# S5's entering states by one instruction for both directions, turned by ScalarE; a late bias on ScalarE; a pad of 448 bytes

## The chip, the cores and the metric

The kernel runs on one core of a Trainium2 chip. The metric is the device time of one execution in microseconds (us), the median of several runs. TensorE (PE) multiplies and loads weights (PEld), VectorE (DVE) and GpSimd (POOL) do elementwise work, ScalarE (ACT) does activations and copies, and SyncE (SP) issues nearly all DMAs. On-chip memory (SBUF) has 128 partitions; a tile is a rectangle in it. PE writes into PSUM banks, which ACT and DVE empty.

## The reference

One layer of a diffusion backbone for 256 context tokens and 2048 latent tokens, width 1024. Two parts of it matter here, S5 and the matrix products.

```
def s5_scan(u, a_re, a_im, log_dt, b_re, b_im, c_re, c_im, s0_re, s0_im):
    ...
    a_cum, h = lax.associative_scan(compose, (a_seq, bu), axis=1)
    h = h + a_cum * lax.complex(s0_re, s0_im)[:, None]
    y = jnp.einsum('gcp,btgp->btgc', lax.complex(c_re, c_im), h).real
    return y, h[:, -1]

def trunk_layer(x, cond, hg_s0, s5_s0_re, s5_s0_im, P, l):
    ada = jnp.dot(jax.nn.silu(cond), P['ada_w'][l]) + P['ada_b'][l]
    sh1, sc1, g1, sh2, sc2, g2 = jnp.split(ada[:, None, :], ADA_CHUNKS, axis=-1)
    h = rms_norm(x, P['norm1_g'][l]) * (1.0 + sc1) + sh1
    mix, hg_end, s5_re, s5_im = token_mixing(h, hg_s0, s5_s0_re, s5_s0_im, P, l)
    x = x + g1 * mix
    h = rms_norm(x, P['norm2_g'][l]) * (1.0 + sc2) + sh2
    x = x + g2 * jnp.dot(jnp.square(jax.nn.relu(jnp.dot(h, P['mlp_w1'][l]))), P['mlp_w2'][l])
```

`s5_mixer` calls `s5_scan` once forwards and once on the flipped sequence, for 16 groups of 16 channels with a complex state of 64. `token_mixing` ends in a product with `w_out`.

## The kernel before

Tokens go in five blocks: block 0 is the 256 context tokens, blocks 1 to 4 are 512 latent tokens each. Every large product is split in three: an operand is held as a rounded `hi` and a remainder `lo`, and `gemm_cm` (lines 186 to 194) issues hi by hi, lo by hi and hi by lo for each of 8 slices of the width, 24 matmuls into one PSUM bank. One such bank is called a unit below. Its weights (`whl`, four buffers) are loaded by `load_unit`, rounded by ACT (L156), and the remainder is subtracted by DVE (L162) or POOL (L160). The moving operand, which is streamed through PE, is a pair of `hi` and `lo` tiles of 128 by 512.

The program has three stages. Until about 700 us, pass 1 makes the normalised inputs and the recurrent part HGRN2, and the S5 tables. From about 700 to 1070 us four things share the engines: `pass2` (the rest of the input products), `s5_ctx` and `s5_lat` (S5), `ada_late` (16 of the 24 adaLN chunk pairs, which aren't needed at the start), and the output product and MLP of block 0. After that the MLP of block 0 ends and blocks 1 to 4 follow: each has `mix_out` (8 units with `w_out`, each emptied by DVE at L1225), and four quarters of `mlp_up` (8 units, emptied by ACT at L1241, squared by DVE at L1242, split by ACT at L1244 and DVE at L1245) and `mlp_down` (8 units, emptied by DVE at L1257 with the same kind of instruction as L1225).

Where the moving operands lie: pass 1 and 2 keep theirs in the pool `hp`, block 0's MLP in `h30`. In blocks 1 to 4, `mix_out` and `mlp_up` read theirs from the pool `h3a`, and `mlp_down` reads the hidden layer from `h3b`. `h3a` stands on the left side of memory behind a tile called `pad`, which nothing reads; `h3b`, `h30` and `hp` are placed from the right side. In the program as built, each 512-wide tile of `h3a` starts 1600 bytes past a multiple of 2048 within its partition (the first at byte 134,720), and each of `hp` and `h3b` starts 1984 bytes past one.

`s5_lat` does one of 16 groups at a time (lines 967 to 1023). Partitions 0 to 63 carry the forward direction, 64 to 127 the backward one, which ACT turned round when it emptied PSUM (L990, L991), so that both scan forwards. Per group: POOL makes phase tables (L322 to L327), DVE rotates the input by four products and two sums (L997, L1001, L1002), scans real and imaginary part (L1005), DVE and POOL rotate back (L997). Then `hh`, the state that enters each step, is written: DVE copies the first state for each direction (L1010, L1011), and for real and imaginary part one subtraction or addition for each half of the partitions (L1013, L1014), the lower one with a reversed order. PE multiplies `hh` with the output tables (L1018 to L1020), ACT empties that into `yl` (L1021).

`ada_unit` multiplies the condition with one pair of adaLN chunks into the only bank of `pb` (L647), ACT copies the rows (L650), PE turns them (L652), and DVE adds the bias into `adaT` (L653). Only then is the bank free for the next unit or for another user.

The engines' queues run in order. The order of all instructions on each engine is set when the program is built, by the framework's scheduler from a simulated timeline, so an edit in one place can move others around it.

Of the kernel before, what the change touches and what calls it, by code (L numbers as in the profile page):

```python
# [10 lines left out]
F32 = mybir.dt.float32  # L11
F32R = mybir.dt.float32r
I32 = mybir.dt.int32
AF = mybir.ActivationFunctionType
# [20 lines left out]
JL = LAT // S5L  # L35
# [39 lines left out]
def trunk_kernel(ctx, tc, I, O):  # L75
# [12 lines left out]
    def nm(s):  # L88
        uid[0] += 1
        return f"{s}_{uid[0]}"  # L90
# [7 lines left out]
    def pb():  # L98
        return psums["b"].tile([128, 512], F32, tag="pb", name=nm("pb"))
# [19 lines left out]
    adab = const("adab", [128, 48], I["ada_b"], q=A)  # L119
# [421 lines left out]
    def ada_late(ap_):  # L541
        c32 = cond32(ap_)
        for q in range(16):
            aws = []
            for r in range(2):
                aw = ap_.tile([128, 4, 256], F32, tag="awt", name=nm("awt"), bufs=2)
                SP.dma_start(aw, I["ada_w1"][q, :, 4 * r:4 * r + 4, :])
                aws.append(aw)
            ada_unit(pb(), aws, c32, ap_, slice(16 + 2 * q, 18 + 2 * q))
            if q == 11:  # L550
                for c in range(2):
                    V.scalar_tensor_tensor(gs2[:, c, :], adaT[:, 32:40, c], 1.0, n2g, ALU.add, ALU.mult)
            yield
# [85 lines left out]
        G.tensor_copy(c32[:, :, 0:2], csil)  # L639
        return c32  # L640

    def ada_unit(pt, aws, c32, rpool, blocks):


        for r in range(2):
            for j in range(4):
                PE.matmul(pt[32 * j:32 * j + 32, 0:256], c32[:, 4 * r + j, :], aws[r][:, j, :],  # L647
                          start=r == 0, stop=r == 1)
        row = rpool.tile([128, 256], F32, tag="row", name=nm("row"))
        A.activation(row, pt[:, 0:256], AF.Copy)  # L650
        for j in range(2):
            PE.matmul(pt[:, 256 + 2 * j:258 + 2 * j], row[:, j * 128:(j + 1) * 128], sel, start=True, stop=True)  # L652
        V.tensor_tensor(adaT[:, blocks, :], pt[:, 256:260].rearrange("p (j c) -> p j c", j=2),  # L653
                        adab[:, blocks].unsqueeze(2).to_broadcast([128, 2, 2]), ALU.add)

# [294 lines left out]
    def s5_lat(sp, s0):  # L950
# [4 lines left out]
        for q in range(4):  # L955
# [10 lines left out]
            for gq in range(4):  # L966
# [27 lines left out]
                def rot(a, dve):  # L994
                    m = [w(f"m{i}", 1 if i < 3 else 2) for i in range(4)]
                    for i, (x, y_) in enumerate(((0, pr), (1, pi), (1, pr), (0, pi))):
                        (V if i in dve else G).tensor_tensor(m[i], a[:, x, :], y_, ALU.mult)  # L997
                    return m
# [5 lines left out]
                for ri in range(2):  # L1004
                    V.tensor_tensor_scan(gg[:, ri, :], rt8[:, g:g + 1].to_broadcast([128, JL]), m[2 * ri],  # L1005
                                         s0[:, ri, g:g + 1], ALU.mult, ALU.add)
                m = rot(gg, ROT[1])
                hh = sp.tile([128, 2, JL], F32, tag="hh", name=nm("hh"), bufs=2)
                e = JL - 1
                V.tensor_copy(hh[0:64, :, 0], s0[0:64, :, g])  # L1010
                V.tensor_copy(hh[64:128, :, e], s0[64:128, :, g])  # L1011
                for ri, (x, y_, op) in enumerate(((m[0], m[1], ALU.subtract), (m[2], m[3], ALU.add))):
                    V.tensor_tensor(hh[0:64, ri, 1:JL], x[0:64, 0:e], y_[0:64, 0:e], op)  # L1013
                    V.tensor_tensor(hh[64:128, ri, 0:e][:, ::-1], x[64:128, 0:e], y_[64:128, 0:e], op)  # L1014
                ps = pdd()
                for a in range(2):
                    as_ = slice(128 * a, 128 * a + 128)
# [282 lines left out]
    def pool(stack, name, bufs=1, side="left"):  # L1300
        return stack.enter_context(tc.tile_pool(name=name, bufs=bufs, side=side))
# [179 lines left out]
    p3 = pool(e5, "p3")  # L1481
    with ExitStack() as e:
        s5_out(1, pool(e, "so1"))
    pad = pool(e5, "pad").tile([128, 16], F32, tag="pad", name="pad")
    G.memset(pad, 0.0)
    h3a = pool(e5, "h3a", 9)
    fs = mlp_up(0, 3, h2, p30, h30, none)
# [129 lines left out]
```

## Time and profile before

| | us |
|---|---|
| median of 3 runs | 2869.47 |
| lowest, highest | 2864.01, 2870.82 |
| profiled execution | 2862.84 |
| its span | 2860.9 |
| PE busy in the span | 2708.4 (95%) |
| DVE busy | 1887.5 (66%) |
| ACT busy | 1108.4 (39%) |

The span runs from the first to the last instruction of the profiled execution. PE's busy share counts pipelined matmuls, so a busy PE isn't yet a PE at its peak: how many matmuls it gets through in a stretch has to be read beside it. From 1400 us on PE is busy without a break until the last block's end; idle time lies before about 1400 us.

### The profile page before, as it was taken

To read this page: it belongs to the slowest core of one execution; us is meant where nothing else is said; L and a number is where in the kernel's file an instruction comes from. 1 tells how busy PE (TensorE), PEld (TensorE's weight loads), DVE (VectorE), ACT (ScalarE), POOL (GpSimd) and SP (SyncE) were. 2 spreads that over 40 slices of the span, in tenths; PEclk is the share of its full clock that TensorE was granted. 3 is DMA by queue.
4 is the path that set the end of the run, shared out by engine and by line. 5 is a ranking of instruction groups with operands and counts; after the bars stand their busy time and mean duration, and the time that the engine had idled before them with its cause. 6 is when DMAs were issued, how large, how long until landed. Compare 5 with 4: busy or idle time off the path is not lost.

```text
span 2860.9 us, 38042 instructions
## 1 busy us (share of the span) xinstructions
PE 2708.4 (95%) x14376; PEld 2257.5 (79%) x14376; DVE 1887.5 (66%) x2766; ACT 1108.4 (39%) x1710; POOL 920.4 (32%) x809
## 2 busy tenths in 40 slices
PE   6798999899999879999999999999999999999998
PEld 3576878887777679987788888788887888888888
DVE  9879678956899976669873475943474334543336
ACT  4645455532333445442422343333343223423323
POOL 4435334612533533343231232211332111411113
PEclk8899999999999979999999999999999999999999
DMA  7784555688886756533333343333343234233333
GB/s 264 282 294 151 188 193 178 229 286 310 299 295 225 241 173 203 174 118 111 111 103 96 125 143 108 111 99 104 114 149 106 99 94 127 90 124 96 96 96 126
DMA packets 186279, 467.17 MB, mean 163 GB/s; under 512 B 40176, under 2 KB 70000, under 8 KB 173040
## 3 DMA queue, kind: packets, MB, share of 16 engines
q1 hardware_dynamic: 183936, 463.56, 48.8%
q8 instruction: 114, 1.87, 0.3%
q10 hardware_dynamic: 2160, 1.18, 0.1%
q14 instruction: 69, 0.57, 0.1%
HBM read 383.47 MB, written 77.53 MB: 161 GB/s over the span
## 4 chain that ended last, share of the span: by engine, by line
PE 62%; DVE 10%; DMA 2%; issue 1%; ACT 0%; SPq 0%; POOL 0%; DVEq 0%; ACTq 0%
PE pg L194 20%; PE pg L193 20%; PE pg L192 20%; DVE x L1184 3%; DVE m L997 1%; DVE whl L162 1%; DMA awt<-in_ada_w_dram 1%; DVE gg L1005 1%; DVE pa L289 0%; PE pb L1051 0%; DVE hh L1014 0%; DVE hh L1013 0%; DVE lo L304 0%; DMA t<-mixD 0%; PE pd L986 0%
## 5 line engine op out<-in xcount | busy, mean ns | idle before, releaser
L192 PE MATMUL pg<-hi,whl 128*128 128x512 f32 (+1 forms) x3488 | 1286.5, 371 | 10.2 <-ACT st L586 4.9
L194 PE MATMUL pg<-hi,whl 128*128 128x512 f32 (+1 forms) x3488 | 1286.2, 370 | 8.4 <-DVE whl L162 8.4
L193 PE MATMUL pg<-lo,whl 128*128 128x512 f32 (+1 forms) x3488 | 1287.0, 370 | 2.3 <-DVE lo L1245 2.3
L160 POOL TENSOR_TENSOR whl<-wraw,whl 128x512 fp32r<-128x512 f32 (+1 forms) x296 | 435.7, 1493 | 1193.5 <-ACT whl L156 1159.9
L192 PEld LDWEIGHTS pg<-hi,whl 128*128 128x128 f32 x3488 | 662.3, 190 | 130.6 <-issue 5.8
L194 PEld LDWEIGHTS pg<-hi,whl 128*128 128x128 f32 x3488 | 662.9, 190 | 125.8 <-DVE whl L162 8.9
L193 PEld LDWEIGHTS pg<-lo,whl 128*128 128x128 f32 x3488 | 663.4, 190 | 120.0 <-issue 6.9
L156 ACT ACTIVATE whl<-wraw 128x1024 fp32r<-128x1024 f32 (+1 forms) x396 | 415.3, 1051 | 588.1 <-PE pg L194 457.0
L162 DVE TENSOR_TENSOR whl<-wraw,whl 128x1024 fp32r<-128x1024 f32 x248 | 310.7, 1254 | 63.1 <-ACT whl L156 61.8
L1257 DVE SCALAR_TENSOR_TENSOR x<-pg,adaT,x 128x512 f32<-128x512 f32 (+1 forms) x168 | 111.8, 669 | 282.9 <-PE pg L194 282.4
L1242 DVE TENSOR_TENSOR t<-t 128x512 f32<-128x512 f32 (+1 forms) x160 | 114.1, 714 | 261.0 <-ACT t L1241 260.3
L1241 ACT ACTIVATE t<-pg 128x512 f32<-128x512 f32 (+1 forms) x160 | 88.7, 554 | 382.3 <-PE pg L194 379.6
L1184 DVE SCALAR_TENSOR_TENSOR x<-x,cvw 128x512 f32<-128x512 f32 (+1 forms) x300 | 216.3, 764 | 0.6
L1245 DVE TENSOR_TENSOR lo<-t,hi 128x512 fp32r<-128x512 f32 (+1 forms) x160 | 142.5, 891 | 35.0 <-ACT hi L1244 34.8
L791 POOL TENSOR_TENSOR kt<-kt,tnx 64x256 f32<-64x256 f32 (+1 forms) x120 | 100.9, 848 | 163.6 <-issue 126.4
L252 POOL TENSOR_TENSOR sq<-sq,sq 128x512 f32<-128x512 f32 (+1 forms) x56 | 87.3, 1559 | 125.6 <-ACT sq L248 125.6
L1244 ACT ACTIVATE hi<-t 128x512 fp32r<-128x512 f32 (+1 forms) x160 | 92.8, 581 | 82.1 <-DVE t L1242 82.1
L1225 DVE SCALAR_TENSOR_TENSOR x<-pg,adaT,x 128x512 f32<-128x512 f32 (+1 forms) x40 | 27.8, 694 | 110.9 <-PE pg L194 110.8
L248 ACT ACTIVATE sq<-x 128x512 f32<-128x512 f32 (+1 forms) x120 | 66.0, 553 | 75.9 <-DVE sq L252 17.4
L787 PE MATMUL psc<-qzr,kt 128*128 128x128 f32 x576 | 74.6, 281 | 10.7 <-DVE kt L791 7.0
L787 PEld LDWEIGHTS psc<-qzr,kt 128*128 128x128 f32 x576 | 70.4, 196 | 14.4 <-POOL kt L791 7.8
L303 ACT ACTIVATE hi<-hm,adaT 128x512 fp32r<-128x512 f32 (+1 forms) x72 | 49.5, 697 | 68.5 <-DVE hm L301 64.5
(373 smaller groups left out, 2919.6 us busy)
## 6 DMA issues: line engine op xcount, KB each, us to landing
wraw<-in_mlp_w_dram SPq DMA_DIRECT2D x328, 512.0 KB, 3.5
whl<-w_p2c_hl SPq DMA_DIRECT2D x32, 1024.0 KB, 7.6
whl<-w_p1c_hl SPq DMA_DIRECT2D x22, 1024.0 KB, 7.7
wraw<-in_w_out_dram SPq DMA_DIRECT2D x40, 512.0 KB, 3.6
awt<-in_ada_w_dram SPq DMA_DIRECT2D x32, 512.0 KB, 5.9
whl<-w_p1t_hl SPq DMA_DIRECT2D x12, 1024.0 KB, 4.9
x<-in_xT_dram SPq DMA_DIRECT2D x16, 512.0 KB, 6.4
aw<-in_ada_w_dram SPq DMA_DIRECT2D x8, 1024.0 KB, 7.2
```

The source lines that it names most:

```text
L156: A.activation(hi[:, :w], raw[:, :w], AF.Copy)
L160: G.tensor_tensor(lo[:, h_], raw[:, h_], f32(hi[:, h_]), ALU.subtract)
L162: V.tensor_tensor(lo[:, :w], raw[:, :w], f32(hi[:, :w]), ALU.subtract)
L192: PE.matmul(ps[:, :n], wh, xh[:, ts], start=k == 0, stop=False)
L193: PE.matmul(ps[:, :n], wh, xl[:, ts], start=False, stop=False)
L194: PE.matmul(ps[:, :n], wl, xh[:, ts], start=False, stop=k == 7)
L787: PE.matmul(sc[:, s_], kt[:, s_], z[:, s_], start=True, stop=True)
L791: eng.tensor_tensor(kv, kv, tb(lo_, hi_, 1 - half)[:, hs_, :], ALU.mult)
L1184: V.scalar_tensor_tensor(acc[i][:, :n], u2[:, i, k:k + n], cvw[:, i, k:k + 1], acc[i][:, :n], ALU.mult, ALU.add)
L1242: V.tensor_tensor(r, r, r, ALU.mult)
L1245: V.tensor_tensor(lo, r, f32(hi), ALU.subtract)
L1257: V.scalar_tensor_tensor(x8[:, o, ts], ps[:, :n], adaT[:, 40 + o, c:c + 1], x8[:, o, ts], ALU.mult, ALU.add)
```

## The change

In `s5_lat` a new tile `sq` (in the two buffers of the tag `d`, which `d2` and `gg` use as well) takes the entering states of both directions in scan order: ACT copies the first state (one instruction), DVE does one subtraction and one addition over all 128 partitions. Two copies by ACT bring it into `hh`, the upper half turned round. DVE has 2 instructions per group where it had 6; ACT has 3 more.

`ada_unit` gets an argument for the engine. `ada_late` passes ACT, which adds the bias by two activations (one per chunk) in place of DVE's one addition. The first 8 units stay as they were.

The tile `pad` grows from 64 to 448 bytes per partition. That moves `h3a` up by 384 bytes: in the changed program its 512-wide tiles start 1984 bytes past a multiple of 2048 (the first at byte 135,104), as those of `hp` and `h3b` do in both programs. No other moving operand moves, and the order of instructions doesn't depend on it.

```diff
@@ -546,7 +546,7 @@
                 aw = ap_.tile([128, 4, 256], F32, tag="awt", name=nm("awt"), bufs=2)
                 SP.dma_start(aw, I["ada_w1"][q, :, 4 * r:4 * r + 4, :])
                 aws.append(aw)
-            ada_unit(pb(), aws, c32, ap_, slice(16 + 2 * q, 18 + 2 * q))
+            ada_unit(pb(), aws, c32, ap_, slice(16 + 2 * q, 18 + 2 * q), A)
             if q == 11:
                 for c in range(2):
                     V.scalar_tensor_tensor(gs2[:, c, :], adaT[:, 32:40, c], 1.0, n2g, ALU.add, ALU.mult)
@@ -639,7 +639,7 @@
         G.tensor_copy(c32[:, :, 0:2], csil)
         return c32
 
-    def ada_unit(pt, aws, c32, rpool, blocks):
+    def ada_unit(pt, aws, c32, rpool, blocks, eng=None):
 
 
         for r in range(2):
@@ -650,6 +650,10 @@
         A.activation(row, pt[:, 0:256], AF.Copy)
         for j in range(2):
             PE.matmul(pt[:, 256 + 2 * j:258 + 2 * j], row[:, j * 128:(j + 1) * 128], sel, start=True, stop=True)
+        if eng is A:
+            for j, o in enumerate(range(blocks.start, blocks.stop)):
+                A.activation(adaT[:, o, :], pt[:, 256 + 2 * j:258 + 2 * j], AF.Identity, bias=adab[:, o:o + 1])
+            return
         V.tensor_tensor(adaT[:, blocks, :], pt[:, 256:260].rearrange("p (j c) -> p j c", j=2),
                         adab[:, blocks].unsqueeze(2).to_broadcast([128, 2, 2]), ALU.add)
 
@@ -1005,13 +1009,15 @@
                     V.tensor_tensor_scan(gg[:, ri, :], rt8[:, g:g + 1].to_broadcast([128, JL]), m[2 * ri],
                                          s0[:, ri, g:g + 1], ALU.mult, ALU.add)
                 m = rot(gg, ROT[1])
+
+                sq = sp.tile([128, 2, JL], F32, tag="d", name=nm("sq"), bufs=2)
                 hh = sp.tile([128, 2, JL], F32, tag="hh", name=nm("hh"), bufs=2)
                 e = JL - 1
-                V.tensor_copy(hh[0:64, :, 0], s0[0:64, :, g])
-                V.tensor_copy(hh[64:128, :, e], s0[64:128, :, g])
+                A.activation(sq[:, :, 0], s0[:, :, g], AF.Copy)
                 for ri, (x, y_, op) in enumerate(((m[0], m[1], ALU.subtract), (m[2], m[3], ALU.add))):
-                    V.tensor_tensor(hh[0:64, ri, 1:JL], x[0:64, 0:e], y_[0:64, 0:e], op)
-                    V.tensor_tensor(hh[64:128, ri, 0:e][:, ::-1], x[64:128, 0:e], y_[64:128, 0:e], op)
+                    V.tensor_tensor(sq[:, ri, 1:JL], x[:, 0:e], y_[:, 0:e], op)
+                A.activation(hh[0:64], sq[0:64], AF.Copy)
+                A.activation(hh[64:128], sq[64:128, :, ::-1], AF.Copy)
                 ps = pdd()
                 for a in range(2):
                     as_ = slice(128 * a, 128 * a + 128)
@@ -1481,7 +1487,7 @@
     p3 = pool(e5, "p3")
     with ExitStack() as e:
         s5_out(1, pool(e, "so1"))
-    pad = pool(e5, "pad").tile([128, 16], F32, tag="pad", name="pad")
+    pad = pool(e5, "pad").tile([128, 112], F32, tag="pad", name="pad")
     G.memset(pad, 0.0)
     h3a = pool(e5, "h3a", 9)
     fs = mlp_up(0, 3, h2, p30, h30, none)
```

The built programs differ in their order only between about 710 and 1200 us of the run. On DVE, towards the end of S5: `gg` is the scan, `m` its rotated parts, `hh` and `sq` the entering states, `whl` a weight split, `x` and `pg` the output product of block 0, `adaT` the bias. Lines from 650 on stand up to 6 lower in the numbering after the change. Before:

```order
L1005 SCALAR_TENSOR_TENSOR gg_9116<-rt_132,s_5238,m_1409_9106 128x256
L1005 SCALAR_TENSOR_TENSOR gg_9116<-rt_132,s_5238,m_1411_9108 128x256
L997 TENSOR_TENSOR m_1414_9119<-gg_9116,ph_9087 128x256
L1225 SCALAR_TENSOR_TENSOR x_1337_8789<-pg_9173,adaT,x_1337_8789 128x256
L997 TENSOR_TENSOR m_1415_9120<-gg_9116,ph_9087 128x256
L653 TENSOR_TENSOR adaT<-pb_8491,adab 128x4
L162 TENSOR_TENSOR whl_9463<-wraw_9461,whl_9463 128x1024
L1013 TENSOR_TENSOR hh_9127<-m_1414_9119,m_1415_9120 64x255
L1014 TENSOR_TENSOR hh_9127<-m_1414_9119,m_1415_9120 64x255
L1013 TENSOR_TENSOR hh_9127<-m_1416_9121,m_1417_9122 64x255
L1014 TENSOR_TENSOR hh_9127<-m_1416_9121,m_1417_9122 64x255
```

After:

```order
L1231 SCALAR_TENSOR_TENSOR x_1349_8805<-pg_9189,adaT,x_1349_8805 128x256
L1009 SCALAR_TENSOR_TENSOR gg_9132<-rt_132,s_5238,m_1422_9122 128x256
L252 TENSOR_TENSOR sq_9221<-sq_9221,sq_9238 128x256
L1009 SCALAR_TENSOR_TENSOR gg_9132<-rt_132,s_5238,m_1424_9124 128x256
L162 TENSOR_TENSOR whl_9479<-wraw_9477,whl_9479 128x1024
L1001 TENSOR_TENSOR m_1427_9135<-gg_9132,ph_9103 128x256
L1001 TENSOR_TENSOR m_1428_9136<-gg_9132,ph_9103 128x256
L252 TENSOR_TENSOR sq_9221<-sq_9221,sq_9241 128x256
L1018 TENSOR_TENSOR sq_9143<-m_1429_9137,m_1430_9138 128x255
L1018 TENSOR_TENSOR sq_9143<-m_1427_9135,m_1428_9136 128x255
```

The bias of an adaLN unit stood on DVE between the rotation and a weight split, and is gone; four half-width instructions have become two of full width, further ahead of the next group.

The same place on ACT: `row` is an adaLN unit, `u`, `d` and `yl` are S5's input, rotated input and output. Before:

```order
L650 ACTIVATE row_8500<-pb_8491 128x256
L156 ACTIVATE whl_9463<-wraw_9461 128x1024
L983 ACTIVATE u_9341<-pd_9338 128x256
L248 ACTIVATE sq_9225<-x_1337_8789 128x256
L990 ACTIVATE d_9346<-pd_9343 64x512
L991 ACTIVATE d_9346<-pd_9343 64x512
L650 ACTIVATE row_8647<-pb_8638 128x256
L1021 ACTIVATE yl_8933<-pd_9134 128x16x16
```

After:

```order
L248 ACTIVATE sq_9238<-x_1349_8805 128x256
L156 ACTIVATE whl_9479<-wraw_9477 128x1024
L1016 ACTIVATE sq_9143<-s_5238 128x2
L987 ACTIVATE u_9357<-pd_9354 128x256
L248 ACTIVATE sq_9241<-x_1349_8805 128x256
L994 ACTIVATE d_9362<-pd_9359 64x512
L995 ACTIVATE d_9362<-pd_9359 64x512
L269 ACTIVATE rcol_9247<-pa_9244,epsb 128x2
L1019 ACTIVATE hh_9144<-sq_9143 64x512
L1020 ACTIVATE hh_9144<-sq_9143 64x512
```

The two copies into `hh` (L1019, L1020) stand behind the next group's `d`, and the adaLN units have ended before this place.

At the end of S5 on DVE: `t`, `lo` belong to block 0's `mlp_up`, `x` with `posr` or `posc` is the position signal of block 1, `gt` is S5's last part. Before:

```order
L1245 TENSOR_TENSOR lo_9494<-t_9490,hi_9493 128x256
L1245 TENSOR_TENSOR lo_9588<-t_9584,hi_9587 128x256
L1242 TENSOR_TENSOR t_9622<-t_9622 128x256
L1245 TENSOR_TENSOR lo_9626<-t_9622,hi_9625 128x256
L240 TENSOR_TENSOR x_1765_11418<-x_1765_11418,posr 128x512 x2
L240 TENSOR_TENSOR x_1765_11418<-x_1765_11418,posc 128x512 x2
L1242 TENSOR_TENSOR t_9659<-t_9659 128x256
L1043 TENSOR_SCALAR gt_11078<-gt_11078 128x512
L1044 TENSOR_TENSOR gt_11078<-gt_11078,yo_11076 128x512
L162 TENSOR_TENSOR whl_9672<-wraw_9670,whl_9672 128x1024
```

After:

```order
L1251 TENSOR_TENSOR lo_9642<-t_9638,hi_9641 128x256
L162 TENSOR_TENSOR whl_9757<-wraw_9755,whl_9757 128x1024
L1248 TENSOR_TENSOR t_9675<-t_9675 128x256
L1251 TENSOR_TENSOR lo_9679<-t_9675,hi_9678 128x256
L162 TENSOR_TENSOR whl_9788<-wraw_9786,whl_9788 128x1024
L1248 TENSOR_TENSOR t_9715<-t_9715 128x256
L1251 TENSOR_TENSOR lo_9719<-t_9715,hi_9718 128x256
L1263 SCALAR_TENSOR_TENSOR x_1349_8805<-pg_9722,adaT,x_1349_8805 128x256
L1263 SCALAR_TENSOR_TENSOR x_1349_8805<-pg_9754,adaT,x_1349_8805 128x256
L240 TENSOR_TENSOR x_1781_11434<-x_1781_11434,posr 128x512 x2
L240 TENSOR_TENSOR x_1781_11434<-x_1781_11434,posc 128x512 x2
L1263 SCALAR_TENSOR_TENSOR x_1349_8805<-pg_9785,adaT,x_1349_8805 128x256
```

The four additions of the position signal stood among the units of `mlp_up`; now the remaining weight splits and two evictions of `mlp_down` (L1263, L1257 before) come first.

## Rows read from the trace of the kernel before

**Rows 1.** The page, part 1: busy time and share of each engine.

```profile
PE 2708.4 (95%) x14376; PEld 2257.5 (79%) x14376; DVE 1887.5 (66%) x2766; ACT 1108.4 (39%) x1710; POOL 920.4 (32%) x809
```

**Rows 2.** Windows of the S5 stage: length; busy of PE, PEld, DVE, ACT, POOL; clock; DMA.

```profile
738.00:790.00 52.00, 48.58 (x262) 37.80 (x261) 45.31 (x77) 20.49 (x36) 28.92 (x37) 0.97 0.86 304
790.00:890.00 100.00, 90.28 (x588) 69.85 (x587) 99.08 (x161) 25.33 (x51) 39.00 (x42) 1.00 0.82 280
890.00:930.00 40.00, 40.00 (x263) 32.31 (x264) 34.81 (x49) 19.22 (x38) 14.17 (x15) 0.96 0.61 203
930.00:1030.00 100.00, 85.79 (x597) 72.12 (x596) 95.39 (x159) 42.64 (x79) 44.75 (x46) 0.86 0.58 186
1030.00:1070.00 40.00, 28.26 (x173) 25.21 (x173) 30.31 (x36) 17.02 (x30) 20.56 (x14) 0.79 0.72 259
```

**Rows 3.** Waits of PE, 738 to 1070: total us, times, longest.

```profile
PE pd L1019 <- DVE hh L1014: 10.2, 8, 2.3
PE pg L194 <- DVE whl L162: 8.4, 2, 5.2
PE pb L647 <- DVE adaT L653: 5.3, 2, 4.8
...
PE pg L192 <- ACT whl L156: 3.4, 2, 2.3
...
PE pd L1020 <- DVE hh L1014: 1.1, 1, 1.1
```

**Rows 4.** DVE groups by form, 700 to 1070: count, busy us, mean ns, idle before.

```profile
L1014 DVE TENSOR_TENSOR hh<-m,m 64x255 f32<-64x255 f32 x32 | 23.9, 747 | 0.5
...
L1013 DVE TENSOR_TENSOR hh<-m,m 64x255 f32<-64x255 f32 x32 | 19.2, 602 | 0.4
...
L1010 DVE COPY hh<-s 64x2 f32<-64x2 f32 x16 | 4.4, 278 | 3.2 <-PE pd L1020 3.2
...
L1011 DVE COPY hh<-s 64x2 f32<-64x2 f32 x16 | 3.8, 235 | 0.3
...
L653 DVE TENSOR_TENSOR adaT<-pb,adab 128x4 f32<-128x4 f32 x16 | 2.4, 150 | 1.4 <-PE pb L652 1.3
...
L1001 DVE TENSOR_TENSOR m<-m,m 128x256 f32<-128x256 f32 x16 | 7.7, 483 | 0.0
...
L1002 DVE TENSOR_TENSOR m<-m,m 128x256 f32<-128x256 f32 x16 | 6.6, 413 | 0.0
```

**Rows 5.** ACT groups by form, 700 to 1070.

```profile
L991 ACT ACTIVATE d<-pd 64x512 f32<-64x512 f32 x16 | 9.5, 593 | 0.2
...
L990 ACT ACTIVATE d<-pd 64x512 f32<-64x512 f32 x16 | 9.4, 590 | 23.4 <-PE pd L986 23.4
...
L1155 ACT ACTIVATE ws<-ol 128x512 f32<-128x512 f32 x8 | 5.1, 632 | 28.8 <-DVE ol L1153 28.8
...
L269 ACT ACTIVATE rcol<-pa,epsb 128x2 f32<-128x2 f32 x1 | 0.3, 262 | 0.0
```

**Rows 6.** DVE timeline in `mlp_down` of block 1: start, length.

```profile
1520.80 0.75 DVE L1257 SCALAR_TENSOR_TENSOR x<-pg,adaT,x 128x512 f32<-128x512 f32 x1 [2.99 <-PE pg L194]
...
1526.24 0.75 DVE L1257 SCALAR_TENSOR_TENSOR x<-pg,adaT,x 128x512 f32<-128x512 f32 x1 [3.07 <-PE pg L194]
```

**Rows 7.** DVE timeline in `mix_out` of block 2.

```profile
1620.48 0.75 DVE L1225 SCALAR_TENSOR_TENSOR x<-pg,adaT,x 128x512 f32<-128x512 f32 x1 [3.15 <-PE pg L194]
...
1626.08 0.75 DVE L1225 SCALAR_TENSOR_TENSOR x<-pg,adaT,x 128x512 f32<-128x512 f32 x1 [3.23 <-PE pg L194]
```

**Rows 8.** PE alone, four windows of 20 us: busy (matmuls), clock, DMA share.

```profile
102.00:122.00 20.00, 20.00 (x90) 1.00 0.78 282
1514.00:1534.00 20.00, 20.00 (x90) 1.00 0.34 106
1616.00:1636.00 20.00, 20.00 (x88) 1.00 0.29 90
1560.00:1580.00 20.00, 20.00 (x88) 1.00 0.25 79
```

## The prediction

> **What bounds the kernel now.** I read the page's busy shares first, then windows over the stage that the S5 and adaLN edits touch, then the waits of PE in it, and last the spacing of PE's units in the stages behind it, where the pad acts.
>
> PE is the bound, 2708.4 of 2860.9 us busy [rows 1], so a gain must either fill PE's idle time or make its matmuls follow each other faster. The windows [rows 2] show where PE is idle: 3.4 us in 738 to 790, 9.7 in 790 to 890, none in 890 to 930, 14.2 in 930 to 1030 and 11.7 in 1030 to 1070, 39 us together. Beside that, the granted clock is 0.86 in the fourth window and 0.79 in the fifth, that is, PE spent a part of them at 1.2 in place of 2.4 GHz after pauses; busy time multiplied by what is missing from 1.0 gives 1.5, 0, 1.6, 12.0 and 5.9 us, 21 us of work done slowly. So 60 us is all that this stage can give back. In 790 to 890 DVE is busy for 99.1 of 100 us and in 930 to 1030 for 95.4, while ACT has 25.3 and 42.6: there DVE is what PE waits for. By name [rows 3], PE waits 10.2 and 1.1 us for DVE's `hh`, 5.3 for DVE's `adaT`, 8.4 for DVE's weight split L162: 25.0 us.
>
> After 1070 us the spacing of units counts. A unit is always 24 matmuls, and its eviction on DVE follows its last one. In `mlp_down` evictions start at 1520.80 and 1526.24, 5.44 us apart [rows 6]; in `mix_out` at 1620.48 and 1626.08, 5.60 apart [rows 7]. Both evictions are the same kind of instruction, wait for PE (DVE idle 3 us before each), take their weights from the same four buffers and have no idle PE: 20 us hold 90 matmuls in `mlp_down` and 88 in `mix_out`, with PE busy for all 20 at clock 1.00 [rows 8]. `mlp_up`, whose evictions are on ACT, also has 88. What `mix_out` and `mlp_up` share, and `mlp_down` doesn't, is the pool of the moving operand: `h3a`. Pass 1, which streams from `hp`, has 90 as `mlp_down` does [rows 8]. So the slow spacing goes with `h3a`, and the one thing that I find different about `h3a` is where it starts: 1600 bytes past a multiple of 2048, where `hp` and `h3b` start 1984 past.
>
> **The pad.** After the change `h3a` starts 1984 past as well. It feeds 8 units of `mix_out` and 32 of `mlp_up` in each of four blocks, 160 units, each 0.16 us shorter if it takes the spacing of the others: 25.6 us, all of it on PE, which is busy without a break there. The bounds: nothing, if the spacing belongs to these two stages for another reason; 25.6 us, if it belongs to the start address. A loss would take a third spacing; two pools at the new offset both show the fast one, so I exclude it. I take 25.6, since `mix_out` differs from `mlp_down` in nothing else that I can find.
>
> **The entering states.** Removed from DVE: 32 and 32 half-width instructions (23.9 and 19.2 us) and 32 copies (4.4 and 3.8), together 51.3 us [rows 4]. Added: 32 instructions of 128 by 255. Their price lies between 413 ns (L1002, the same form on 128 by 256) and 747 (L1014, in whose place they stand) [rows 4], so 13.2 to 23.9 us; they stand at the place of L1013 and L1014 (602 and 747 ns), so I take 650 ns, 20.8 us. DVE saves 30.5 us, 1.9 per group.
>
> ACT gets three more instructions per group. The two copies of 64 by 512 are bounded by L990's 590 ns (same shape, from PSUM) and L1155's 632 (SBUF to SBUF, 128 by 512) [rows 5]: about 0.61 each. The first state, 128 by 2, is nearest to L269's 262 ns. That is 1.5 us per group, 23.7 in all. The first state depends on nothing late, so on the path from the scan to PE stand two DVE instructions (1.3 us) and two copies (1.2), 2.5 us in place of L1013, L1014 twice over (2.7): no longer than before, and DVE reaches each group's end 1.9 us sooner for every group in front of it in a full stretch. Of the nine waits for `hh`, 11.3 us in all and 1.26 each [rows 3], I take 7 as gone. Behind a copy that waits for DVE stand ACT's weight split L156 and the emptying of PSUM, so a late `sq` now delays these too; and `sq` shares two buffers with `d2` and `gg`, so the next group's scan waits for ACT's copies. Between the two stand six rotations and sums of the next group, 6 times 0.45 to 0.6 us, which covers the copies while ACT isn't behind.
>
> Bounds of this edit and its consequences: at best the 25.0 us of waits for DVE and the 21 of slow clock go, 46 us; at worst the copies, 1.2 us for each of 16 groups, come on top of PE's waits, a loss of 19.5.
>
> **The late bias.** DVE loses 16 instructions, 2.4 us [rows 4]; ACT gets 32 of 128 by 2, at L269's 262 ns 8.4 us [rows 5]. What counts is that L653 stood in DVE's full queue behind a rotation while PE waited for the bank of `pb`: 5.3 us, 4.8 of it at one place [rows 3]. On ACT the bias follows the turning with little in front of it, and in the new order all 16 units end before that place. I take 5 us. The bounds are the 5.3 and a loss of 0.3 per unit, 5 us, if ACT's two instructions and what stands before them keep the bank longer. ACT's added work, 32 us on 124.7 of 332 [rows 2], leaves it under half busy, which hides its own cost.
>
> **The end of S5.** PE waits 8.4 us for two weight splits [rows 3]. In the order before, the second of the two splits at that place stands behind four additions of the position signal; now those additions follow the splits of `mlp_up` and two evictions. The additions still form one block, and later units need splits behind it, so I take half, 4 us, between none and 8.4.
>
> S5, bias and end: 7 + 5 + 4 = 16 us. Clock regained and new waits for ACT are set against each other, some 4 us each, within the bounds.
>
> **The sum.** The profiled execution took 2862.84 us, 1.9 more than its span. 2862.8 - 25.6 - 16 = 2821.2. The median of the runs, 2869.47, is 6.6 above the profiled one; with that, 2828.
>
> **A rule that speaks against it.** Rows 6 to 8 show two spacings at the same clock and shape. The Trainium skill, page "TensorE: Matmul & The Clock Gate", section "Back-to-back issue gap", makes the gap between matmuls depend on the number of columns alone, and "SBUF — State Buffer", section "Who interferes with whom", lets PE never wait for another engine. By these a move by 384 bytes is worth nothing. The trace doesn't agree with the first as it stands, since at 512 columns it shows 5.44 and 5.60 us per 24, but a cause other than the address would save the rule. That is the first rival.
>
> **Rivals.**
>
> 1. The spacing belongs to the stage, not to the address (what else runs then, or the pool's side of memory), and the pad does nothing. For it: no row shows `h3a` at another place. Against it: `mix_out` and `mlp_down` differ only in the pool. Then 2862.8 - 16 = 2847, by the median 2853.
>
> 2. The S5 and bias edits give nothing: DVE's time is given back as waits for ACT, whose queue is in order and now stands in the chain of each group. For it: the path from scan to PE is as long as before (2.5 against 2.7 us). Against it: ACT is at 25 to 43% and DVE full. Then the pad alone: 2837, by the median 2844.
>
> 3. Slower: ACT becomes the bound of the S5 chain. Place: the copies into `hh` behind `d` and weight splits, with PE's L1019 and the next scan waiting for them. Price: 16 times 1.5 us for the group and 16 times 0.5 for the bias, 32 us on the path, while DVE's saving doesn't reach it. It decides from the point where a group comes more than 25.6 / 16 = 1.6 us later than before, because the pad's gain is then used up; at 32 us the time is 2869, by the median 2876. Against it: ACT's share.
>
> **How the numbers follow.** Forecast 0.72, rival 1 0.13, rival 2 0.10, rival 3 0.05. The forecast's own range: S5, bias and end between nothing much and twice the estimate, 2808 to 2844. Rival 1 reaches from 2837 to 2869; I take the part up to 2852. Range 2804 to 2852, which leaves out about half of rival 1, rival 3 and the far end of the clock's return. A measurement of this kernel can tell about 0.3%, 8.6 us, from no change. Faster by more than that: the forecast, rival 2 and about two thirds of rival 1, 0.91. Within it: the rest of rival 1 and half of rival 3, 0.06. Slower: 0.03.
>
> **What will show it.** The pad: evictions of `mix_out` and `mlp_up` 5.44 us apart, 90 matmuls in 20 us. If they stay at 5.60, rival 1 holds. The entering states: waits of PE for `hh` below 5 us in total, now named for ACT; DVE's busy time in the S5 stage lower by some 33 us. The bias: no wait of PE for `adaT` above 1 us. The end: the waits for L162 between the last S5 group and `mix_out` of block 1 halved. The forecast is wrong if PE's idle time and slow clock before 1100 us haven't shrunk by 10 us, or if the spacing hasn't changed.

## The result and the profile after

| | us |
|---|---|
| before, median of 4 runs | 2867.93 (2864.01 to 2870.82) |
| after, median of 4 runs | 2836.14 (2834.27 to 2838.19) |
| ratio, 95% interval | 0.989 (0.9873 to 0.9907) |
| after, profiled execution | 2838.19, span 2836.2 |

The change is worth 31.8 us by the medians. The forecast was 2828, a gain of 41, in a range of 2804 to 2852.

The first part of the page after, to be held against [rows 1]: PE's busy time is 10.3 us less, the span 24.7 less, DVE's busy time 37 less, ACT's 28 more.

```profile
PE 2698.1 (95%) x14376; PEld 2265.1 (80%) x14376; DVE 1850.5 (65%) x2686; ACT 1136.6 (40%) x1790; POOL 917.7 (32%) x809
```

The pad's part. Two of the windows of 20 us of [rows 8], after (length; busy of PE, PEld, DVE, ACT, POOL with counts; clock; DMA share, GB/s), and two evictions of `mix_out` of block 2, which answer to [rows 7]:

```profile
1616.00:1636.00 20.00, 20.00 (x90) 16.57 (x89) 5.46 (x6) 6.32 (x8) 9.17 (x7) 1.00 0.28 93
1560.00:1580.00 20.00, 20.00 (x90) 16.57 (x89) 8.11 (x10) 7.38 (x11) 2.99 (x2) 1.00 0.35 105
```

```profile
1611.39 0.75 DVE L1231 SCALAR_TENSOR_TENSOR x<-pg,adaT,x 128x512 f32<-128x512 f32 x1 [2.99 <-PE pg L194]
1616.83 0.75 DVE L1231 SCALAR_TENSOR_TENSOR x<-pg,adaT,x 128x512 f32<-128x512 f32 x1 [3.07 <-PE pg L194]
```

90 matmuls in place of 88 in both, and 5.44 us from one eviction to the next in place of 5.60. `mlp_up`, at 1560, follows suit.

The S5 stage: the same five windows as in [rows 2].

```profile
738.00:790.00 52.00, 49.39 (x278) 38.95 (x280) 39.19 (x65) 25.57 (x48) 25.23 (x31) 1.00 0.85 303
790.00:890.00 100.00, 97.24 (x628) 73.76 (x628) 94.08 (x140) 37.87 (x85) 42.20 (x44) 0.98 0.85 288
890.00:930.00 40.00, 35.04 (x235) 29.02 (x237) 31.47 (x46) 19.56 (x43) 19.69 (x22) 0.96 0.64 233
930.00:1030.00 100.00, 87.06 (x629) 72.96 (x622) 81.88 (x128) 57.12 (x115) 45.10 (x46) 0.90 0.55 181
1030.00:1070.00 40.00, 30.77 (x199) 25.57 (x198) 32.08 (x38) 16.85 (x29) 19.22 (x13) 0.83 0.75 267
```

PE's idle time is 2.6, 2.8, 5.0, 12.9 and 9.2 us, 32.5 together, and its slow work (busy time by what the clock lacks of 1.0) 17.3: 50 us lost where it was 60. DVE is busy for 278.7 us, 26 less. In its waits, to be held against [rows 3], the names have changed:

```profile
PE pb L1057 <- DVE yo L1052: 7.6, 2, 6.8
PE pd L990 <- ACT u L987: 5.2, 1, 5.2
PE pd L1025 <- ACT hh L1020: 5.0, 4, 2.6
PE pb L647 <- DMA awt<-in_ada_w_dram: 4.0, 4, 1.8
...
PE pg L194 <- DVE whl L162: 1.7, 1, 1.7
```

The wait for `adaT` (5.3) is gone, that for the weight split L162 fell from 8.4 to 1.7, and `hh` costs 5.0 in place of 11.3. New are 7.6 for `yo` (S5's last step, on DVE) and 5.2 for `u` (S5's input, on ACT). The groups that answer to [rows 4] and [rows 5], on DVE and on ACT:

```profile
L1018 DVE TENSOR_TENSOR sq<-m,m 128x255 f32<-128x255 f32 x32 | 19.3, 624 | 0.2
...
L1020 ACT ACTIVATE hh<-sq 64x512 f32<-64x512 f32 x16 | 10.0, 628 | 0.2
L1019 ACT ACTIVATE hh<-sq 64x512 f32<-64x512 f32 x16 | 10.0, 628 | 40.8 <-DVE sq L1018 40.8
...
L655 ACT ACTIVATE adaT<-pb,adab 128x2 f32<-128x2 f32 x32 | 6.6, 259 | 11.8 <-PE pb L652 11.7
L1016 ACT ACTIVATE sq<-s 128x2 f32<-128x2 f32 x16 | 3.2, 202 | 11.5 <-DVE m L1001 11.5
```

The prices lie within 5% of the estimates (650, 610 and 262 ns), but for the first state, 202 ns in place of 262.

One thing of the profiled execution has to be known before it is compared. By 640 us, where the order is still that of before, the same DVE instructions come 5.9 us later than in the execution of before, and the granted clock is lower in it (windows of 500 to 700 us: before, after, and the kernel of experiment 1 with the pad alone):

```profile
500.00:700.00 200.00, 183.26 (x1301) 162.46 (x1300) 156.47 (x336) 77.92 (x154) 77.98 (x101) 0.98 0.76 270
```

```profile
500.00:700.00 200.00, 187.20 (x1264) 167.49 (x1264) 157.52 (x343) 79.59 (x158) 74.59 (x101) 0.93 0.74 265
```

```profile
500.00:700.00 200.00, 187.18 (x1263) 166.34 (x1265) 156.63 (x337) 77.69 (x153) 74.75 (x101) 0.93 0.75 265
```

It isn't owed to the change: the order there is the same in all kernels, and in the run with S5 and bias alone the delay is 0.4 us. Executions differ here: the clock of this window is 0.93 with the pad alone and with the entering states alone (experiment 2) as well, and 0.96 to 0.98 in others with either pad. So gains in traces below are counted between equal instructions of two traces, from a point behind it; the windows of the S5 stage above lie at fixed times and contain this delay.

### The profile page after: what moved, and what is told of

The parts are those of the page before. It is cut to its first block, busy times and chain, and to the rows that moved or that the text cites. A ratio compares the mean times of both kernels' runs of the same rounds, so it can differ in the third digit from the quotient of the medians.

```text
span 2836.2 us, 38037 instructions
## 1 busy us (share of the span) xinstructions
PE 2698.1 (95%) x14376; PEld 2265.1 (80%) x14376; DVE 1850.5 (65%) x2686; ACT 1136.6 (40%) x1790; POOL 917.7 (32%) x809
## 4 chain that ended last, share of the span: by engine, by line
PE 67%; DVE 14%; DMA 2%; issue 1%; ACT 1%; SPq 0%; POOL 0%; DVEq 0%; ACTq 0%
PE pg L193 20%; PE pg L194 20%; PE pg L192 20%; DVE x L1190 4%; DVE m L1001 1%; DVE whl L162 1%; PE psc L791 1%; DMA t<-mixD 1%; DVE kt L795 1%; DMA x<-uD 1%; DVE q L796 1%; DVE Sl L860 1%; DVE gg L1009 0%; DVE q L797 0%; DVE at L812 0%
## 5 line engine op out<-in xcount | busy, mean ns | idle before, releaser
L162 DVE TENSOR_TENSOR whl<-wraw,whl 128x1024 fp32r<-128x1024 f32 x248 | 311.9, 1258 | 63.2 <-ACT whl L156 62.2
L1263 DVE SCALAR_TENSOR_TENSOR x<-pg,adaT,x 128x512 f32<-128x512 f32 (+1 forms) x168 | 111.8, 669 | 282.4 <-PE pg L194 281.7
```

The source lines that it names most:

```text
L162: V.tensor_tensor(lo[:, :w], raw[:, :w], f32(hi[:, :w]), ALU.subtract)
L1263: V.scalar_tensor_tensor(x8[:, o, ts], ps[:, :n], adaT[:, 40 + o, c:c + 1], x8[:, o, ts], ALU.mult, ALU.add)
```

## The experiments

Times are medians of their runs; "before" ran on the same chip each time, so each has its own ratio to it.

**1. S5 and bias alone, and the pad alone.**

```diff
-    pad = pool(e5, "pad").tile([128, 112], F32, tag="pad", name="pad")
+    pad = pool(e5, "pad").tile([128, 16], F32, tag="pad", name="pad")
```

in the changed kernel for the first; the reverse in the kernel before for the second.

> The changed kernel with the pad as it was (64 bytes), so only the entering states and the late bias are changed; the order of instructions is that of the changed kernel. Theory (the forecast): the pad carries most, and this kernel gains the 16 us that the prediction gives to S5, bias and end; by the trace of after, where matched instructions come 12 to 13 us sooner over the S5 stage, 2855 +- 5 us, with mix_out and mlp_up of blocks 1 to 4 at 5.60 us per unit. Rival: the spacing belongs to the order of work, then this kernel is as fast as the changed one, 2836, and its units stand 5.44 apart. Second rival: the S5 edits give nothing, 2868.

> The kernel before with the pad of 448 bytes and nothing else; its order of instructions is that of before. Theory: 20 us less than before (the trace of after shows PE's matmuls from 1100 us on gaining 20 us, not the predicted 25.6, since the units of blocks 1 and 2 that run while DVE is full give some back): 2848, units 5.44 apart. Prediction's own term: 2842. Rival (the pad does nothing): 2868, units 5.60 apart.

S5 and bias alone: 2855.58 against 2866.47, ratio 0.9959 (0.9945 to 0.9973). The pad alone: 2848.60, ratio 0.9933 (0.9915 to 0.9952). The product of the two is 0.9892, the change's 0.989: the parts add up. The same window of 20 us in the first and in the second kernel:

```profile
1616.00:1636.00 20.00, 20.00 (x87) 16.11 (x86) 5.46 (x6) 5.88 (x8) 7.47 (x5) 1.00 0.32 104
```

```profile
1616.00:1636.00 20.00, 20.00 (x90) 16.57 (x89) 6.36 (x7) 6.14 (x8) 9.26 (x6) 1.00 0.35 104
```

87 matmuls with the pad of 64 bytes (a regular stretch holds 88), 90 with 448. With the pad alone the time from the first eviction of `mix_out` of block 1 to the last of `mlp_up` of block 4 falls from 1596.3 to 1576.0 us, by 20.3. In the other kernel the gain stands at 8.3 us at 1120 us and hardly moves to the end (7.2 at 2720); that is less than the 10.9 between the medians, because the profiled execution of before, 2862.84, is one of its faster ones. So both rivals of the first run fall, and so does that of the second. The forecast's division holds; both sizes are below it.

**2. The entering states without the bias.**

```diff
-            ada_unit(pb(), aws, c32, ap_, slice(16 + 2 * q, 18 + 2 * q), A)
+            ada_unit(pb(), aws, c32, ap_, slice(16 + 2 * q, 18 + 2 * q))
```

> The entering states alone: pad of 64 bytes, and the late bias again one addition on DVE. Theory: the bias is worth the 5 us that PE waited for adaT, so this comes out 5 us above the kernel with states and bias, about 2860, with a wait of PE for adaT of several us in its trace. Rival: another wait (for yo, or for u from ACT, both new in the trace of after) sets the end of the stage anyway, and the bias is worth nothing: 2855. Rival: the states edit alone loses by its three instructions on ACT: 2870 or more.

2857.07, ratio 0.9963 (0.9949 to 0.9977): 1.5 us above the kernel with the bias, with overlapping ranges (2853.7 to 2858.2, and 2851.0 to 2857.9). Yet the wait for `adaT` is back:

```profile
PE pb L1057 <- DVE yo L1052: 7.6, 2, 6.9
PE pb L647 <- DVE adaT L657: 6.4, 4, 3.2
...
PE pd L990 <- ACT u L987: 3.0, 2, 2.8
...
PE pd L1025 <- ACT hh L1020: 1.8, 3, 1.4
```

In the kernel of experiment 1, with the bias on ACT:

```profile
PE pd L1025 <- ACT hh L1020: 6.2, 4, 2.7
PE pd L990 <- ACT u L987: 5.1, 1, 5.1
```

6.4 us came for `adaT`, while `u` and `hh`, both on ACT, cost 4.8 us where they cost 11.3 with the bias on ACT. A wait for DVE was exchanged for waits for ACT. The rival that the bias is worth nothing holds, as far as 1.5 us can be told.

**3. The address by itself.** This kernel has nothing but the loop of `gemm_cm`, with a start that moves by 8 elements (32 bytes) from unit to unit:

```diff
+    for x in range(0, 512, 8):
+        p = bank()
+        unit(p, x, 272)
+        V.tensor_copy(ev[:, 8 * n[0]:8 * n[0] + 8], p[:, 0:8])
```

> Leaves out the whole layer and only issues units of 24 matmuls as gemm_cm does (weights hi, hi, lo; moving operand xh, xl, xh; 512 columns), with nothing else on the chip but an 8-column copy per unit on DVE. First 40 units at offset 1984 (mod 2048) to warm up, then the moving operand's start goes through a 2048-byte stretch in steps of 32 bytes (64 units, from 128 mod 2048), then the weights' start in the same steps, then the moving operand again with 256 columns, then the distance between xh and xl from 2048 bytes up. Theory: the spacing follows from the moving operand's start: 5.60 us at 1600 mod 2048 and 5.44 at 1984, in a pattern that repeats within the stretch. Rival: by itself no offset matters, all units stand the same distance apart (5.44 or less), and the 5.60 comes from something that runs beside it in the layer.

The copies behind the units at 1568 and 1600, and then behind those at 1952 and 1984 (start, length; DVE's idle time before):

```profile
487.77 0.17 DVE L114 COPY ev<-pg 128x8 f32<-128x8 f32 x1 [5.44 <-PE pg L102]
493.37 0.17 DVE L114 COPY ev<-pg 128x8 f32<-128x8 f32 x1 [5.43 <-PE pg L102]
...
554.79 0.17 DVE L114 COPY ev<-pg 128x8 f32<-128x8 f32 x1 [5.43 <-PE pg L102]
560.25 0.17 DVE L114 COPY ev<-pg 128x8 f32<-128x8 f32 x1 [5.30 <-PE pg L102]
```

5.60 and 5.46 us, with nothing else running but these copies; in the layer it is 5.60 and 5.44, and the warm-up units of this kernel, all at 1984, stand 5.44 apart too. Over the 2048 bytes the pattern repeats every 256: 5.46 at 192 past a multiple of 256, 5.50 at 0, and 5.60 to 5.62 at the other six. The same holds for the weights' start (5.45 at 192, 5.51 at 128, others 5.59 to 5.61). With 256 columns it is another pattern: 2.87 us at 192 and 2.72 at 128. The rival falls: the address alone does it. The kernel was executed once, but the pattern stands in it eight times.

**4. Pairs of starts.** The same kernel, again executed once, with all pairs of 8 starts.

> Leaves out the whole layer, as the first sweep. Units of 24 matmuls for all pairs of 8 starts of the weights and 8 of the moving operand in steps of 32 bytes (weights 64 to 288, moving 128 to 352 past a multiple of 256 is one period), with 512 columns and then with 256; then the moving start alone in steps of 4 bytes; then the lo weights alone shifted in steps of 32 bytes. Theory: the spacing is a property of the pair (weights' start, moving operand's start) modulo 256, so the best moving start shifts with the weights' start, and with 256 columns it lies elsewhere than with 512. Rival: each address has a good value of its own (192 for both), whatever the other is. If a pair below 5.44 us for 512 columns exists, the layer could be faster still.

Mean ns from one matmul to the next at 512 columns, worked out from the starts in the trace (rows: weights, columns: moving operand, both past a multiple of 256):

```
          0     32     64     96    128    160    192    224
  0   227.8  233.5  229.1  233.9  233.5  233.9  233.5  233.0
 32   233.0  227.8  233.5  229.1  233.0  232.2  233.9  233.5
 64   233.0  233.0  227.0  233.5  229.6  233.9  233.0  233.9
 96   234.3  233.5  233.5  227.8  233.5  228.7  233.9  233.5
128   233.5  233.9  233.5  233.0  227.8  233.5  229.6  233.9
160   233.9  233.5  234.3  233.5  232.6  227.8  233.5  229.1
192   229.1  233.9  233.5  233.9  233.0  233.0  227.8  233.5
224   233.5  229.1  233.9  233.5  234.3  233.0  233.0  227.0
```

The pair decides: equal residues are fast, a moving operand 64 further is second, all others are slow. No pair is below 227, the layer's fast spacing (5.44 us per 24), so in steps of 32 bytes the layer has nothing more to win at 512 columns. With 256 columns five of eight rows have their best value (113.5 to 114.8) where the moving operand lies 64 below the weights, but three do not (117.8 there); weights at 192 with moving at 128, 113.5 in the first sweep, gave 117.8 here, at the same addresses. What else enters there stays open, and so does what in the chip makes the starts matter.

The Trainium skill, page "TensorE: Matmul & The Clock Gate", section "Back-to-back issue gap", goes by the number of columns: at 512 it gives about 131 ns as measured for a stream of weight loads and matmuls, and about 216 ns for the isolated gap of one matmul. The sweeps agree with neither: they show 227 to 234 at a granted clock of 1.00 with a weight load for each matmul, and a difference of 3% by the starts alone. For this loop the measurement decides.

**5. The roles exchanged in the layer.**

```diff
+    padw = wts.tile([128, 32], F32, tag="padw", name="padw")
+    nc.gpsimd.memset(padw, 0.0)
...
-    pad = pool(e5, "pad").tile([128, 16], F32, tag="pad", name="pad")
+    pad = pool(e5, "pad").tile([128, 48], F32, tag="pad", name="pad")
```

> The kernel before with a pad of 128 bytes ahead of the weights, so that the four buffers of whl start 64 past a multiple of 256 and no longer 192, and the pad before h3a at 192 bytes, so that h3a starts at 64 past as in the kernel before; hp and h3b stay at 192. Theory (the spacing belongs to the pair of starts; equal residues are fast at 512 columns): the roles are exchanged, mix_out and mlp_up at 5.44 us per unit, mlp_down and pass 1 at 5.60 or near it. Rival (192 is a good start by itself): nothing changes for mlp_down (5.44), and mix_out and mlp_up stay at 5.60.

Pass 1, `mlp_down` and `mix_out`, in that order (compare [rows 8]):

```profile
102.00:122.00 20.00, 20.00 (x87) 16.22 (x88) 19.56 (x27) 8.55 (x13) 12.33 (x8) 1.00 0.81 289
1514.00:1534.00 20.00, 20.00 (x88) 16.08 (x87) 5.46 (x6) 4.25 (x4) 5.10 (x4) 1.00 0.22 79
1616.00:1636.00 20.00, 20.00 (x90) 16.57 (x89) 6.23 (x7) 6.32 (x8) 7.99 (x7) 1.00 0.33 106
```

They changed places: the evictions of `mix_out` stand 5.44 apart, those of `mlp_down` 5.60. The single run took 2863.11. No start is good by itself; the pair theory holds in the layer.

**6. Why 20 and not 25.6 us.** The kernel before with a cut convolution, once with each pad:

```diff
-        for k in range(1, CONV_K):
+        for k in range(1, 2 if b >= 2 else CONV_K):
```

> The kernel before, with the convolution of blocks 2 to 4 cut to 2 of its 31 taps (29 are left out, 174 instructions on DVE at L1184), so that DVE is no longer full in 1280 to 1480 and 1680 to 1870 us; pad of 64 bytes. It is the reference point for the next run. In the kernel before, PE's units there stand up to 12 us apart where DVE is full. Theory: without the taps these stretches run at PE's pace, the kernel is some 10 to 20 us faster than before, and all its units of mix_out and mlp_up stand 5.60 apart.

> The same with the pad of 448 bytes. Theory: the pad gained 20 us and not 25.6 because DVE was full beside two or three quarters of mlp_up; with the taps gone the difference to the run with 64 bytes, counted between equal instructions from 1200 us to the end, grows to 24 to 25.6 us. Rival: the gain per unit is smaller than 0.16 us in all irregular quarters, whatever DVE does, and the difference stays at 20.

2862.77 and 2836.76 (ratios 0.9985 and 0.9901 to before): 26.0 us apart where the pad alone was worth 17.9 by medians (24.1 and 19.2 by the ratios). The windows 1280 to 1480, first with the whole convolution (before, the pad alone), then with the cut one (64 and 448 bytes):

```profile
1280.00:1480.00 200.00, 194.98 (x842) 156.97 (x840) 184.91 (x229) 67.64 (x90) 57.69 (x29) 1.00 0.34 110
```

```profile
1280.00:1480.00 200.00, 193.99 (x847) 157.74 (x846) 186.19 (x232) 66.97 (x90) 60.08 (x28) 1.00 0.35 113
```

```profile
1280.00:1480.00 200.00, 200.00 (x865) 161.59 (x864) 103.98 (x121) 70.13 (x94) 46.48 (x30) 1.00 0.35 114
```

```profile
1280.00:1480.00 200.00, 200.00 (x876) 163.59 (x875) 102.98 (x119) 70.03 (x94) 46.48 (x30) 1.00 0.36 114
```

With DVE at 185 of 200 us the pad brings 5 matmuls more and PE's idle time grows from 5.0 to 6.0 us; with DVE at 104 PE isn't idle and the pad brings 11. From the first eviction of `mix_out` of block 1 to the last of `mlp_up` of block 4 the time falls from 1590.5 to 1567.1 us, so the pad is now worth 23.5 us, against 20.3. Other traces with the whole convolution put the latter at 21.3: this stretch takes 1596.3 to 1597.4 us in three of them with 64 bytes and 1574.6 to 1576.4 in six with 448. So DVE's load accounts for 2 to 3 of the 4 to 5 us that were missing. The rest lies mainly in the first two quarters of blocks 1 to 3, without a cause shown. Two things expected of the cut kernel were wrong: it brought 6 us (4 by the ratio) and not 10 to 20, and not all its units stand 5.60 apart. The second quarter of `mlp_up` in blocks 1 to 3 still takes 44.3 us from its first to its last eviction where a regular one takes 39.3; 18 matmuls of the convolution's norm and of S5's output come in between.

**7. The end of S5.** In the trace of after DVE's queue shows what `yo` waits behind, and PE's row what it costs:

```profile
1048.80 2.13 DVE L240 TENSOR_TENSOR x<-x,posr 128x512 f32<-128x512 f32 x2
1050.85 3.20 DVE L240 TENSOR_TENSOR x<-x,posc 128x512 f32<-128x512 f32 x2
1053.97 0.47 DVE L1263 SCALAR_TENSOR_TENSOR x<-pg,adaT,x 128x256 f32<-128x256 f32 x1
1054.36 1.09 DVE L1049 TENSOR_SCALAR gt<-gt 128x512 f32<-128x512 f32 x1
1055.48 0.69 DVE L1050 TENSOR_TENSOR gt<-gt,yo 128x512 f32<-128x512 f32 x1
1056.87 0.90 DVE L1052 TENSOR_TENSOR yo<-yo,gt 128x512 f32<-128x512 f32 x1 [0.70 <-ACT gt L1051]
```

```profile
1057.83 1.22 PE L1057 MATMUL pb<-yo,gluw 128*128 128x512 f32 x1 [6.83 <-DVE yo L1052]
```

The four additions of the position signal, 5.3 us, stood ahead of a weight split in the order before; now they stand ahead of the GLU of S5. In this experiment they are taken from DVE:

```diff
-        x8 = xblock(p3, b, p3_bufs[n])
+        x8 = xblock(p3, b, p3_bufs[n], engs=(G,) if b == 1 else None)
```

> The changed kernel with block 1's eight additions of the position signal all on POOL instead of half of them on DVE. Theory: at the end of S5 PE waits 6.8 us for yo because four additions (5.3 us) stand in DVE's queue ahead of the GLU's multiplications; without them the wait falls below 2 us and the kernel takes about 2831. Rival: S5's end is held by its own chain (ACT's table load and tanh, DVE's products), and PE's wait or another in its place stays: 2836. Rival: POOL becomes late for weight splits and it is slower.

2837.28, ratio 0.9889 (0.9871 to 0.9908): no gain. The waits:

```profile
PE pg L194 <- DVE whl L162: 5.5, 1, 5.5
PE pb L1057 <- DVE yo L1052: 5.3, 2, 4.3
```

`yo` fell by 2.3 us and the split rose by 3.8. Before, after and here the two together cost 8.4, 9.3 and 10.8 us. The theory of the additions falls: they decide which of the two PE waits for, not how long. What sets the sum was not found; in the kernel of experiment 8 it is 5.4.

**8. The turned copy on POOL.**

```diff
-                A.activation(hh[64:128], sq[64:128, :, ::-1], AF.Copy)
+                G.tensor_copy(hh[64:128], sq[64:128, :, ::-1])
```

> The changed kernel with the turned copy of the entering states (hh, partitions 64 to 127) on POOL instead of ACT. Theory: PE's waits for hh (5.0 us) and u (5.2 us), both on ACT, come from ACT's queue, in which the copies stand; with one of them gone these fall by half, and the kernel gains some 4 us, 2832. Rival: POOL takes longer for the copy (in order behind the phase tables) and the path to PE grows: 2840 or more, with waits of PE for hh named for POOL.

2833.96, ratio 0.9881 (0.9863 to 0.9900); the changed kernel's range (2834.3 to 2838.2) overlaps with its 2829.9 to 2838.7. The wait for `u` has shrunk by more than half, that for `hh`, now named for POOL, only from 5.0 to 3.8, and others have come:

```profile
PE pa L263 <- DVE sq L252: 4.2, 1, 4.2
PE pd L1025 <- POOL hh L1020: 3.8, 2, 2.9
PE pg L194 <- DVE whl L162: 3.4, 1, 3.4
...
PE pb L1057 <- DVE yo L1052: 2.0, 1, 2.0
...
PE pd L990 <- ACT u L987: 1.4, 1, 1.4
```

That ACT's queue caused the wait for `u` agrees with this; that removing it gains 4 us isn't shown.

**9. Block 0's tiles at 128, and both edits together.**

```diff
+    pad0 = pool(e4, "pad0", side="right").tile([128, 16], F32, tag="pad0", name="pad0")
+    G.memset(pad0, 0.0)
     h30 = pool(e4, "h30", 19, side="right")
```

> The changed kernel with a second pad of 64 bytes ahead of block 0's pool h30, so that its 256-wide tiles start 128 past a multiple of 256 and no longer 192. The sweep gave 2.87 us per unit of 256 columns at 192 and 2.72 at 128. Theory: from 1070 to 1200 us PE issues one 256-column matmul after another (836 in 100 us, 119.6 ns each), so this part of about 130 us gets 5% shorter, 6.6 us, and the kernel takes 2829 to 2830. Rival: weights come no faster there (DMA share 0.60, four buffers), and it stays at 2836.

> The changed kernel with h30 at 128 past a multiple of 256 and the turned copy of hh on POOL. Theory: the two gains (3 to 4 us and about 2 us against the changed kernel) lie in neighbouring stretches and add up in part, 2830 +- 4 us. Rival: the waits that end S5 only change names, and it is no better than h30 alone, 2833.

With `h30` at 128: 2832.85 (2829.8 to 2835.9), ratio 0.9877 (0.9860 to 0.9894). By the medians this is 3.3 us below the changed kernel, half of what was expected; the intervals of the ratios overlap, so that no gain is shown. Two windows of this kernel, then the first of them in the changed one:

```profile
1070.00:1090.00 20.00, 20.00 (x178) 20.00 (x178) 14.96 (x20) 12.59 (x21) 5.74 (x5) 1.00 0.69 219
1150.00:1170.00 20.00, 20.00 (x172) 20.00 (x172) 10.26 (x13) 8.37 (x8) 8.61 (x6) 1.00 0.55 181
```

```profile
1070.00:1090.00 20.00, 20.00 (x169) 20.00 (x169) 14.34 (x19) 11.89 (x17) 5.88 (x5) 1.00 0.83 279
```

178 matmuls in 20 us for 169, as the sweep had it, but only 172 at 1150. By the starts in the trace the spacing is 113.3 ns up to 1104 us, some 2 us behind a pause of PE of 1 us, and 117.8 from there to the end of the stretch, though all tiles of `h30` start 128 past a multiple of 256. With both edits it changes between the same two values at the same time. These are the two values that one pair of starts had in the two sweeps: at 256 columns it can take either, and what decides is open.

With both edits: 2830.65 (2829.11 to 2833.02), ratio 0.9877 (0.9862 to 0.9892). All its runs are below all of the changed kernel's, 5.5 us by the medians, though the two were not timed side by side and their intervals against before overlap. By the medians it is the fastest of the kernels tried; by the ratio it equals the one with `h30` alone, so the rival isn't excluded.

## Why the prediction was right, and where it wasn't

**The pad: right in mechanism, some 5 us too large.** The spacing went from 5.60 to 5.44 as forecast, and the address alone does it (experiments 3 and 5). The first rival falls with it. The rule behind it was put too narrowly: what counts is the start of the moving operand against that of the weights; 1984 was good because `whl` starts 1216 past a multiple of 2048, and so 192 past a multiple of 256 like it. The term that was mis-sized is the count: "all of it on PE, which is busy without a break there" was taken for all 160 units. In 1280 to 1480 PE was busy for 195.0 of 200 us. Beside the convolution DVE is at 185 of these 200, and there part of what a shorter unit gains comes back as idle time of PE. It came to 20 to 21 us in place of 25.6, with 2 to 3 us of the difference shown to be DVE's (experiment 6).

**The entering states: right in mechanism.** The gain was put at 7 us. The kernel with states alone gains 10.6 us by its ratio (6.6 to 14.6), within the bounds; that kernel has its own order at the end of S5, so the 10.6 stand against 7 for the states and 4 for the end together, and no run separates the two. The waits for `hh` fell from 11.3 to 5.0 and changed their name from DVE to ACT, as was said. Against that stand 5.2 us for `u`, which ACT makes in the same queue as the copies. That a late `sq` delays ACT's other work was in the text, and some 4 us of new waits for ACT were set against 4 of regained clock; the slow work fell by 3.7 us, so this pair of terms came near.

**The late bias: wrong in size.** 5 us were taken and 1.5 measured, which can't be told from none. The wait for `adaT` went, as forecast; its place was taken by waits for ACT. The term counted a wait of PE as time, while in experiment 2 other waits stand in its place, 6.5 us for 6.4.

**The end of S5: wrong.** Of the 8.4 us half was to go. The wait for the split did (1.7), but the one for `yo` came (7.6). The step that failed is the reading that the wait for the split is owed to the additions ahead of it, so that moving them returns time: experiment 7 takes them away and the two waits cost 10.8 us together. What does hold up this place stays open.

**The sum.** S5, bias and end were put at 16 us; the ratio of the kernel with them gives 11.8 (7.7 to 15.8). The pad was put at 25.6; its ratio gives 19.2 (13.8 to 24.4). The second rival (S5 gives nothing) and the third (ACT makes it slower) fall with experiment 1. That these parts come so near to 16 is in part luck: the terms for the bias and for the end, 9 us together, brought 1.5 us and no gain that shows, and the kernel with the states alone brought 3.6 more than the states' own term. Of the signs that were named, three came clearly: 90 matmuls in 20 us, no `adaT`, L162 more than halved. Two came only just: `hh`, under ACT's name, is at 5.0 and was to be below it (6.2 in the kernel of experiment 1), and idle time and slow clock fell by 10 us (by 8 in that kernel). DVE's time fell by 26 and not by 33 us. One of the signs, the split, was the sign of a gain that wasn't there. In the range a sum is off: 2828 less another 16 is 2812, and not 2808; nothing hangs on it.

## What to carry to other kernels

Where two stages run the same loop at the same clock and one is some per cent slower, compare the start addresses of both matmul operands, and test it with a pad. A gain per unit is to be multiplied only with the units of those stretches where no other engine is full. A wait that is removed counts for no more than what the next wait in the same stretch leaves of it.

## What the runs showed of the hardware

- The spacing of matmuls that each load new weights depends on the starts of both operands, modulo 256 bytes: 227 to 228 ns at equal residues, 229 to 230 with the moving operand 64 further, 232 to 234 otherwise (steps of 32 bytes, 512 columns, clock 1.00; experiment 4).
- In steps of 4 bytes, with the weights at 192, 14 of the 16 starts that are 4 past a multiple of 16 take 235.6 to 239.8 ns, the other two 231.2 and 234.1; the best of all is 192 itself (227.3; experiment 4).
- The second moving operand and the remainder weights count too: `xl` 32 bytes further than a multiple of 256 from `xh` gives 232 ns (experiment 3), `lo` weights 32 bytes off 233 ns (experiment 4), with everything else at equal residues.
- With 256 columns the range is 113.5 to 120 ns and the best pair is another; the same pair gave 113.5 in one sweep and 117.8 in the other, and in the layer 113.3 and, behind a pause, 117.8 (experiment 9).
